# A fused pooling and state-space layer: the sample's scan factors computed at once for all heads, and three sums of squares as products of two parts

## The chip, the cores and the metric

The kernel runs on one core of a Trainium2 chip. The metric is the device time of one execution, in microseconds (us). The engines that matter are TensorE (PE: matmuls, with PEld for its weight loads), VectorE (DVE), ScalarE (ACT) and GpSimd (POOL). SyncE (SP), ACT and POOL also issue DMA transfers. Each engine takes its instructions in an order that is fixed when the kernel is built; where one depends on another engine or on a transfer, it waits for a semaphore.

## The reference, cut to what matters

One layer is computed for two requests that share the weights: a prompt of 256 tokens and a sample of 32 tokens that continues a running stream. All 288 tokens (NT) go through the projections side by side. The part that the change touches is the scan:

```python
xn   = rmsnorm(x, norm_mix_pre)
proj = xn @ w_in                      # u_pool | z | xBC | dt
xbc  = silu(causal_dwconv(xbc))       # -> xs (32 heads of 64), B, C (2 groups)
acum = cumsum(dt * A)                 # per head
lmat = exp(acum_t - acum_s), t >= s   # per head: the "factors"
y    = (lmat * (C B^T)) @ (dt * xs)   # within a request
y   += exp(acum) * (C @ h0)           # sample: state carried in
y    = (y + D * xs) * silu(z)
y    = y * rsqrt(mean(y * y) + eps) * norm_g        # per group of 16 heads
mix  = concat[pool, y] @ w_out
...                                   # then norm, ConvFFN, norm
```

Weights are float32. On the chip every weight tile and every left factor is split into a high part (`hi`, the float32 rounded to the matmul's fp32r type) and the rest (`lo`), and a product is three fp32r matmuls: hi·hi, hi·lo and lo·hi.

## The kernel before, in words

Activations lie with channels over the 128 partitions and the 288 tokens along the free axis. `project()` streams a weight matrix in groups of 256 columns; for each it takes four weight tiles of 128x1024 (`raw`, by DMA on SP), splits them (`whi` by ACT in L138, `wlo` by DVE in L139), and `mm3` issues 24 matmuls of 128x288 per tile (L145 to L147). The order of instructions on each engine is made by a scheduler when the kernel is built; `issue_after`, `high_priority` and `keep_in_program_order` bend it. PE runs matmuls of the projections nearly from end to end; the scan's work is fitted between them.

The scan works on groups of four heads, here called fours (q = 0 to 7). After certain projections (the tables `SCAN_IN` and `SCAN_OUT`, not changed) `scan(i)` does one or both of:

- `four_in(q)`: loads the four's running sums `gb`, its inputs `xw` and its state `h0t`, and forms `ce` and the factors `m`. `m` holds for each of the four heads 256 columns for the prompt's first half, 128 for its second, and 32 for the sample, 416 in all. Twelve Relus (L497: per head 128x256, 128x128 and 128x32), one Exp over 128x1664 (L500) and one product with `cbt` (L502, DVE) make it. `m`, `xw` and `ce` have two buffers each, so the third four's `m` takes the place of the first's.
- `four_out(q)`: sixteen matmuls (L524) in four rounds k: k = 0 and 1 read the prompt's part of `m`, k = 2 the sample's part, k = 3 the state's part (`ce` with `h0t`). They are kept in program order on PE. The first time it runs, two fours go out, q = 0 and q = 1.

`last_in[0]` is the latest DVE instruction that brought a projection's result out of PSUM. `gate_rstd` sums the squares over channels as one float32 matmul with a constant matrix `mean` (L533), twice in the scan; the same is done once more in the last stage (`psum_m`).

```python
four_out(q, ys[2 * n : 2 * n + 2], *got, after=None if n else ready[-1][1][-1])
```

This line of `scan` lets a four's matmuls start only after the product of the last prepared four (`got`, L502) in the order.

## Time and profile before

| What | Value |
|---|---|
| Time, median of 3 runs | 1232.44 us (1232.38 to 1233.84) |
| Profiled execution, its own time | 1231.95 us |
| Span of the profile (first to last instruction) | 1230.2 us |
| PE busy | 1223.2 us, 10037 matmuls |
| DVE busy | 888.5 us |
| ACT busy | 672.2 us |
| POOL busy | 277.8 us |
| First scan output on PE | from 130.12 us |

Times in the trace count from the span's start. A timeline row gives the start, the time taken, the engine, the line of the kernel, what is written from what, the shape and the count; in brackets stands how long the engine had been idle before and what released it. Matmuls overlap, so the distance between two starts is what one costs. A row with a count joins like instructions in sequence. A float32 matmul (not fp32r) appears as two records.

## The change

1. The sample's factors leave `m`, which shrinks from 4 x 416 to 4 x 384 columns (eight Relus in place of twelve, Exp and product over 1536 columns). They are computed once for all eight fours in a tile `ms` (128 x 8 x 32), with the 32 sample tokens of four heads over the 128 partitions: four DMAs on POOL, a subtraction on DVE, Relu and Exp on ACT, three products on DVE, and then four copies on ACT into blocks on the diagonal of a zeroed tile `msz` (32x256 each). Round k = 2 of `four_out` reads `msz` and a small tile `xw_s` of its own.
2. `four_in` is cut in two: the loads stay, the rest becomes `four_mul`. For q = 0 it is called one projection later, behind the third last weight split (`splits[-3]`).
3. The three sums of squares are two fp32r matmuls each, with a high part (a copy on ACT) and the rest (a subtraction on DVE), by `sum_parts`. The constant `mean_r` is a copy on ACT at the kernel's start.

The diff, cut to its core:

```diff
+    mean_r = const.tile([P, P], F32R, name="mean_r")
+    act.activation(mean_r, mean, AF.Copy)
+    def sum_parts(p_, src, pool_, name, last_=True):
+        a = [pool_.tile([P, NT], F32R, tag="sq", bufs=2, name=name) for _ in range(2)]
+        act.activation(a[0], src, AF.Copy)
+        dve.tensor_tensor(a[1], src, a[0].bitcast(F32), op=ALU.subtract)
+        return [(p_, mean_r, a[i], i == 0, last_ and i == 1) for i in range(2)]
...
+    for j in range(4):
+        pool.dma_start(
+            out=ms[NS * j : NS * (j + 1)],
+            in_=g_d.rearrange("(q j) c -> j q c", j=4)[j, :, 384:].unsqueeze(0).broadcast_to([NS, 8, NS]),
+        )
+    def sample_factors():
+        each = lambda t: t.unsqueeze(2).broadcast_to([P, 8, NS])
+        with tc.issue_after(last_in[0].ins):
+            dve.tensor_tensor(ms, each(tok_s[:, 0, :]), ms, op=ALU.subtract)
+            act.activation(ms, ms, AF.Relu)
+            act.activation(ms, ms, AF.Exp, scale=-1.0)
+            for gi in range(2):
+                q4 = slice(4 * gi, 4 * gi + 4)
+                dve.tensor_tensor(ms[:, q4], ms[:, q4], cbs[:, gi : gi + 1, :].broadcast_to([P, 4, NS]), op=ALU.mult)
+            dve.tensor_tensor(ms, ms, each(tok_s[:, 1, :]), op=ALU.mult)
+            for j in range(4):
+                r_ = slice(NS * j, NS * (j + 1))
+                act.activation(msz[r_, j], ms[r_], AF.Copy)
...
-        xw = mp.tile([P, 3, 2 * P], F32, tag="xw", bufs=2, name="xw")
-        sp.dma_start(out=xw[:, 0:2, :], in_=xs_d[:NP_, c].rearrange("(b p) c -> p b c", p=P))
-        sp.dma_start(out=xw[:, 2, :], in_=xs_d[NT - P :, c])
+        xw = mp.tile([P, 2, 2 * P], F32, tag="xw", bufs=2, name="xw")
+        sp.dma_start(out=xw, in_=xs_d[:NP_, c].rearrange("(b p) c -> p b c", p=P))
+        xw_s = mp.tile([P, 64], F32, tag="xw_s", bufs=2, name="xw_s")
+        sp.dma_start(out=xw_s, in_=xs_d[NP_:, c].rearrange("s (j c) -> j s c", j=4))
...
-                for b, (lo_, hi_) in enumerate(((0, 256), (256, 384), (384, MW))):
+                for b, (lo_, hi_) in enumerate(((0, 256), (256, CW))):
...
-                    ops.append((y[:, 256:], xw[:, 2, c], m[:, j, 384:], True, False))
+                    ops.append((y[:, 256:], xw_s, msz[:, j, q, :], True, False))
...
-        ins = pe.matmul(p_, mean, gsum[t], start=True, stop=True)
+        for o, w_, v_, go, end in sum_parts(p_, gsum[t], mp, "gsplit"):
+            ins = pe.matmul(o, w_, v_, start=go, stop=end)
...
+    def four_next(after):
+        q, tiles = loads.pop(0)
+        ready.append((q, four_mul(q, *tiles, after)))
     def scan(i):
+        if loads:
+            four_next((*splits[-3], last_in[0]))
         if i in SCAN_OUT:
...
         if i in SCAN_IN:
-            ready.append((q, four_in(q)))
+            loads.append((q, four_in(q)))
+            if i > 5:
+                four_next((last_in[0],))
+        if i == 6:
+            sample_factors()
```

How the order of instructions changes is shown at three places around the first scan output. In these rows `m`, `xw`, `ce`, `h0t` and `py` are the factors, inputs, state factors, states and results of a four, and `[waits X]` names the engines or transfers whose semaphore an instruction waits for. The line numbers are those of each kernel's own source.

On ACT, before, these rows start with the first Relu of q = 2, whose `m` takes the buffer of q = 0:

```order
L497 ACTIVATE m<-gb,tok 128x256 [waits PE_49]
L497 ACTIVATE m<-gb,tok 128x128
L497 ACTIVATE m<-gb,tok 128x32
L497 ACTIVATE m<-gb,tok 128x256
L497 ACTIVATE m<-gb,tok 128x128
L497 ACTIVATE m<-gb,tok 128x32
L487 ACTIVATE ce<-gb 128x128 [waits PE_49]
```

On ACT, now, from the same Relu on:

```order
L558 ACTIVATE m<-gb,tok 128x256 [waits PE_49]
L558 ACTIVATE m<-gb,tok 128x128
L558 ACTIVATE m<-gb,tok 128x256
L558 ACTIVATE m<-gb,tok 128x128
L558 ACTIVATE m<-gb,tok 128x256
L558 ACTIVATE m<-gb,tok 128x128
L558 ACTIVATE m<-gb,tok 128x256
L558 ACTIVATE m<-gb,tok 128x128
L561 ACTIVATE m<-m 128x1536 [waits Activation_49]
L520 ACTIVATE msz<-ms 32x256 [waits DVE_49]
L520 ACTIVATE msz<-ms 32x256 x3
L548 ACTIVATE ce<-gb 128x128 [waits PE_49]
```

The four copies into `msz` stand behind all eight Relus and the Exp of q = 2, and the first of these Relus waits for PE.

On PE, before, the first four's output, between two projections:

```order
L524 MATMUL py<-m,xw 64x256 [waits DMAHW0_49]
L524 MATMUL py<-m,xw 64x256 x3
L524 MATMUL py<-m,xw 64x128 x4
L524 MATMUL py<-m,xw 64x32 [waits DMAHW1_49]
L524 MATMUL py<-m,xw 64x32 x3
L524 MATMUL py<-ce,h0t 64x32 [waits DMAHW7_49]
L524 MATMUL py<-ce,h0t 64x32 x3
```

On PE, now:

```order
L585 MATMUL py<-m,xw 64x256 [waits DMAHW0_49]
L585 MATMUL py<-m,xw 64x256 x3
L585 MATMUL py<-m,xw 64x128 x4
L585 MATMUL py<-msz,xw_s 64x32 [waits DMAHW1_49,Activation_49,Pool_49]
L585 MATMUL py<-msz,xw_s 64x32 [waits Activation_49] x3
L585 MATMUL py<-ce,h0t 64x32 [waits DMAHW7_49]
L585 MATMUL py<-ce,h0t 64x32 x3
```

The eight matmuls of k = 0 and 1 stand where they stood; the four of k = 2 now each wait for a copy on ACT.

On DVE, before, ahead of the first scan output, from a result brought out of PSUM (`ebuf`) to the split of a weight (`wlo`):

```order
L360 TENSOR_TENSOR ebuf_674<-acc,rstd 128x256 [waits PE_49]
L361 TENSOR_TENSOR ebuf_674<-acc,rstd 128x32
L490 TENSOR_TENSOR ce<-ce,bc 128x128
L493 TENSOR_TENSOR xw<-xw,tok 128x768 [waits DMAHW7_49,DMAHW0_49]
L502 TENSOR_TENSOR m<-m,cbt 128x1664 [waits DMAHW3_49]
L139 TENSOR_TENSOR wlo<-raw,whi 128x1024 [waits Activation_49]
```

On DVE, now, between the same two:

```order
L372 TENSOR_TENSOR ebuf_676<-acc,rstd 128x256 [waits PE_49]
L373 TENSOR_TENSOR ebuf_676<-acc,rstd 128x32
L551 TENSOR_TENSOR ce<-ce,bc 128x128
L554 TENSOR_TENSOR xw<-xw,tok 128x512 [waits DMAHW0_49]
L563 TENSOR_TENSOR m<-m,cbt 128x1536
L551 TENSOR_TENSOR ce<-ce,bc 128x128
L554 TENSOR_TENSOR xw<-xw,tok 128x512 [waits DMAHW7_49]
L563 TENSOR_TENSOR m<-m,cbt 128x1536 [waits DMAHW3_49]
L511 TENSOR_TENSOR ms<-tok_s,ms 128x256 [waits DMASW2_49,DMASW3_49,DMASW1_49,DMASW0_49]
L140 TENSOR_TENSOR wlo<-raw,whi 128x1024 [waits Activation_49]
```

The products of q = 0 moved down to those of q = 1, and with the subtraction for `ms` stand ahead of this `wlo`.

## What the change was predicted to do

> **What bounds the kernel now.** I read the page's busy shares, clock row and chain first, then the waits of PE, then the timelines of PE, ACT and DVE around the places that the change touches. The page:

> ```profile
> span 1230.2 us, 25184 instructions
> PE 1223.2 (99%) x10037; PEld 1212.8 (99%) x10037; DVE 888.5 (72%) x1488; ACT 672.2 (55%) x1013; POOL 277.8 (23%) x428
> PEclk9999999999999999999999999999999999999999
> PE 91%; DVE 3%; ACT 3%; issue 1%; DMA 1%; ACTq 0%; DVEq 0%
> ```

> The waits of PE (what waits, for whom, us in total, times, longest):

> ```profile
> PE idle L261 <- PEq L1316: 0.8, 1, 0.8
> PE psum_f L1223 <- DVE ar L1198: 0.5, 1, 0.5
> PE acc L147 <- DVE wlo L139: 0.4, 1, 0.4
> PE acc L292 <- DVE xs L290: 0.4, 1, 0.4
> PE acc L147 <- DVE wlo L302: 0.4, 1, 0.4
> PE y_ps L1256 <- DVE ar L1250: 0.3, 1, 0.3
> ```

> PE is the bound from end to end: 99% busy, 91% of the chain, the clock full in every slice, and only 2.8 us of waiting in the whole span. So work taken from DVE and ACT is worth nothing by itself; what counts is PE's own matmuls, and whether PE gets a new wait. At 99% any new wait of PE lengthens the span by its full length.

> **Part 1, the sample's factors: the first scan output.** On PE nothing is saved: a 64x32 product stays a 64x32 product, with `msz` for the end of `m`. But round k = 2 now waits for four copies on ACT, and the order of ACT puts these behind eight Relus and the Exp of q = 2. The first of these Relus writes into the buffer of q = 0's `m`, so it waits for PE's last k = 1 matmul of q = 0, the one right ahead of k = 2. So PE must stand still while ACT does all that. Before, the Relus waited in the same way, but nothing that PE needed then was behind them. When PE gets there, from its timeline (weight matmuls, then the first four):

> ```profile
> 127.33 0.29 PE L147 MATMUL acc<-xn,wlo 128*128 128x288 f32 x1
> ...
> 129.90 0.29 PE L147 MATMUL acc<-xn,wlo 128*128 128x288 f32 x1
> 130.12 1.73 PE L524 MATMUL py<-m,xw 128*64 128x256 f32 x24
> 131.67 0.41 PE L524 MATMUL py<-ce,h0t 128*64 128x32 f32 x8
> 131.90 0.63 PE L524 MATMUL py<-m,xw 128*64 128x256 f32 x4
> ```

> From 127.33 to 129.90 there are 21 steps, so 0.1224 us a step. Each float32 product is two records: x24 are the twelve products of k = 0 to 2, x8 the four of k = 3. The latter take 131.90 - 131.67 = 0.23 us; the four of k = 2 have the same size, so k = 2 begins at 131.44 and its last product at 131.61. The last k = 1 product, issued just before 131.44, is done some 0.2 us later, at about 131.64 (estimate from the records' length). What ACT's pieces take, by ACT's timeline:

> ```profile
> 4.66 0.72 ACT L301 ACTIVATE whi<-raw 128x256 fp32r<-128x256 f32 x2 [0.41 <-DMA raw<-in_w_first]
> 7.03 1.03 ACT L301 ACTIVATE whi<-raw 128x256 fp32r<-128x256 f32 x3 [1.20 <-DMA raw<-in_w_first]
> 110.02 1.57 ACT L500 ACTIVATE m<-m 128x1664 f32<-128x1664 f32 x1
> 111.51 0.39 ACT L497 ACTIVATE m<-gb,tok 128x128 f32<-128x128 f32 x1
> ...
> 112.47 0.31 ACT L497 ACTIVATE m<-gb,tok 128x32 f32<-128x32 f32 x1
> 112.68 1.04 ACT L138 ACTIVATE whi<-raw 128x1024 fp32r<-128x1024 f32 x1
> ...
> 132.27 1.90 ACT L497 ACTIVATE m<-gb,tok 128x256 f32<-128x256 f32 x6
> 134.08 0.29 ACT L487 ACTIVATE ce<-gb 128x128 f32<-128x128 f32 x1
> ```

> - Eight Relus: six (two heads of 256, 128, 32) go from 132.27 to 134.08, 0.905 a head. The 32-wide one is 112.68 - 112.47 = 0.21, so a head now costs 0.695, and four 2.78.
> - Exp: 111.51 - 110.02 = 1.49 for 1664 columns, 1.38 for 1536.
> - Four copies of 32x256: no row has this form. The nearest is a 128x256 copy, 0.41 alone and 0.31 for each further one (1.03 - 0.72): 1.34. From below, each at the 0.21 of the 32-column Relu: 0.84.

> The last copy ends at 131.64 + 2.78 + 1.38 + 1.34 = 137.14, and its product, which had started at 131.61, is **5.53 us** late. From below 5.0 (cheap copies). From above 6.2: ACT may reach the first Relu no earlier than in the row at 132.27, 0.63 after 131.64. What DVE and ACT do in that time (splits of the next weights) finishes early and is no loss.

> **The products moved on DVE.** q = 0's products now stand with q = 1's in front of one `wlo`. DVE's rows before:

> ```profile
> 122.62 0.28 DVE L490 TENSOR_TENSOR ce<-ce,bc 128x128 f32<-128x128 f32 x1
> ...
> 123.69 1.88 DVE L502 TENSOR_TENSOR m<-m,cbt 128x1664 f32<-128x1664 f32 x1
> 125.49 1.22 DVE L139 TENSOR_TENSOR wlo<-raw,whi 128x1024 fp32r<-128x1024 f32 x1
> ```

> `ce` and `xw` took 1.07 and `m` 1.80; with 512 and 1536 columns that is 0.2 + 0.6 + 1.67 = 2.47 for a four, so twice 2.47 and 0.33 for the subtraction of `ms` (128x256) make 5.27 against 2.87: this `wlo` ends 2.40 later than 126.71, if DVE starts at the same time. PE first reads it at 127.33, two matmuls later in the new order, 127.57: slack 0.86, so a wait of 1.5 us at worst. But DVE no longer does q = 0's 2.87 us earlier on and so reaches this place earlier, unless it waits there for PE's result: 0 at best. I take 0.2, near the lower end, since the time is given back to the same queue. Two later places (near 160 and 179) have the same shape with one four: 0 to 0.7 together, by the half of this wait; I take 0.1. Sum +0.3.

> **Other steps of part 1 with one answer.** The four loads of `ms` stand on POOL's queue ahead of writes of `xs_d`, and the loads of `xw_s` on SP's among the weights'; both are needed only at about 126 and 131, more than 10 us later, so 0. The copies of `tok_s`, `b_s4`, `dec_s` and `tri_s`, the memset and the Relu and Exp of `ms` lie on ACT and POOL (55% and 23% busy) ahead of 126; 0, and if the Relu of `ms`, which waits for DVE, holds a split behind it, it is inside the 1.5 above. Later fours have shorter products on DVE and ACT.

> **Part 2, the sums of squares.** One of them on PE, with the weight matmuls behind it:

> ```profile
> 212.50 0.65 PE L533 MATMUL psum_g<-gsum,mean 128*128 128x288 f32 x2
> ...
> 213.10 0.29 PE L146 MATMUL acc<-xn,whi 128*128 128x288 f32 x1
> 213.23 0.29 PE L145 MATMUL acc<-xn,whi 128*128 128x288 f32 x1
> 213.92 0.39 PE L147 MATMUL acc<-xn,wlo 128*128 128x288 f32 x1 [0.41 <-DVE wlo L139]
> 214.15 0.29 PE L145 MATMUL acc<-xn,whi 128*128 128x288 f32 x1
> ```

> From 212.50 to 213.10 lie the sum and one weight matmul, 0.60; two fp32r products and that one are three steps, 0.367. So 0.235 less each, **-0.71** for three; 0 if PE must wait for the split instead.

> **Waits that may go.** The rows above show one: 213.23 to 214.15 is 0.92 for two steps of 0.245, 0.67 waited for `wlo`. The other:

> ```profile
> 151.88 0.29 PE L146 MATMUL acc<-xn,whi 128*128 128x288 f32 x1
> 152.26 0.39 PE L147 MATMUL acc<-xn,wlo 128*128 128x288 f32 x1
> 152.48 0.29 PE L145 MATMUL acc<-xn,whi 128*128 128x288 f32 x1
> ```

> 0.60 for two steps, so 0.36. Both are waits for a `wlo` close behind a product of 1664 columns, which is now shorter and, behind a standstill, has time in hand: **-1.03** together if both go, 0 if neither. More than 0.71 + 1.03 = 1.74 can't be gained, since the other waits are not touched.

> **Part 3, the start.** ACT now loads its table and copies `mean_r` between its two loads of `x`:

> ```profile
> 1.25 0.45 ACTq L256 DMA_DIRECT2D xT<-in_x  x1
> 1.74 1.28 ACT L257 ACT_TABLE_LOAD   x1 [1.74 <-PEq L1316]
> xT<-in_x ACTq DMA_DIRECT2D x1, 144.0 KB, 3.5
> ```

> The second load is issued some 1.5 us later (1.28 for the table and 0.2 for the copy) and lands at about 6.3 instead of 1.25 + 3.5 = 4.8. PE's next weights land only at 7.03 (ACT's row above), so 0; 0.5 at most, if `x`'s second part is wanted first.

> **Sum.** 5.53 + 0.3 - 0.71 - 1.03 = +4.1 against the profiled execution of 1231.95 us (its span and 1.75 around it): 1236.0. This execution is 0.49 below the median of the runs, 1232.44, so by the median 1236.5, +0.33%. This case's own range: from 5.0 + 0 - 1.74 = +3.3 (1235.7) to 6.2 + 0.8 - 1.4 = +5.6 (1238.0).

> **Rivals.**

> *The stall costs twice: PE runs at half speed after it.* PE's first matmuls show such a state:

> ```profile
> 0.85 2.90 PE L261 MATMUL idle<-const-float32-1.0 128*128 128x128 f32 x12 [0.85 <-PEq L1316]
> ...
> 5.74 0.50 PE L145 MATMUL acc<-xn,whi 128*128 128x288 f32 x1
> L292 PE MATMUL acc<-xs,raw 128*128 128x288 f32 x4 | 2.0, 644 | 0.4 <-DVE xs L290 0.4
> L533 PE MATMUL psum_g<-gsum,mean 128*128 128x288 f32 x4 | 1.3, 406 | 0.0
> ```

> A float32 record of 128x288 takes 644 ns at the start and 406 in the sums; the fp32r matmul at 5.74 still takes 0.50, later ones 0.29. So PE begins slow, from 0.85 to about 5.7 with 0.4 of waiting, some 4.4 us, while the page's clock digit says full speed there. If a standstill of 5.5 us brings that back, 4.4 us at half rate cost 2.2: 1238.7 (1237.8 to 1239.7). Against it: the trace has no later standstill over 0.5 us, so it can't show one. [...]

> *A wait on DVE ahead of the scan.* If DVE gets to q = 0's products no earlier than before, the full 1.5 us at 127.57 come on top, with the stall unchanged (its start moves with PE): 1236.5 + 1.3 = 1237.8. For it: DVE waits there for PE's result (`ebuf`). Against it: 2.87 us of its earlier work are gone.

> *Not slower: no long standstill.* If the order's wait is met early, because the Relu that waits is satisfied before PE reaches k = 1 (q = 2's `m` in a buffer of its own), the copies end before 131.44 and only the gains are left: 1232.44 - 1.74 + 0.3 = 1231.0, within 0.2%. It decides as soon as the standstill is under 2.46 + 1.44 = 3.9 us, since 2.46 us are 0.2%, about what runs of this kernel can tell from no change. Against it: the order shows the slot wait before and now, and in the row at 132.27 the Relus did begin only after k = 1.

> **How the numbers follow.** Stall with full speed 0.45; with half speed 0.31; DVE's wait on top 0.12; no long standstill, or one cut under 3.9, 0.12. The first gives the time, 1236.5. The range goes from 1234.6, where the last case's upper part ends, to 1239.3, in the half-speed case's upper part; some 0.10 are left out below, 0.06 above. Slower by over 0.2% (above 1234.90) are the first three, 0.86 with a little lost to low ends, given to the last: slower 0.85, same 0.12, faster (below 1229.98) 0.03.

> **What would show it.** In the changed trace: PE idle about 5 us at 131.6, ahead of `py<-msz,xw_s`, released by ACT L520; eight Relus, an Exp and four copies without a gap on ACT between; matmul steps of 0.122 right behind it (0.24 if the half-speed case holds, for some 4 us); no wait for `wlo` near 152 and 213; three sums without float32 records. Wrong I am if copies into `msz` lie before 131, or if PE's waits stay below 4 us in total.

## The result, and the profile after

| | before | changed |
|---|---|---|
| Median | 1232.41 us (1230.74 to 1233.84, 4 runs) | 1238.64 us (1238.0 to 1240.47, 4 runs) |
| Profiled execution, its span | 1231.95, 1230.2 us | 1238.0, 1236.3 us |

The ratio is 1.0059, 95% interval 1.0046 to 1.0071: slower by 0.59%. The forecast was +0.33%, 1236.5 us, with a range up to 1239.3; the median lies near the range's upper end, and the ratio times 1232.44 (1239.7) just above it. The direction and the place were right; the size was too small.

The page of the changed kernel:

```profile
span 1236.3 us, 25196 instructions
PE 1224.2 (99%) x10037; PEld 1214.4 (98%) x10037; DVE 887.5 (72%) x1494; ACT 670.8 (54%) x1000; POOL 287.2 (23%) x436
PEclk9999899999999999999999999999999999999999
PE 93%; DVE 2%; DMA 2%; ACT 1%; issue 1%; SPq 0%; ACTq 0%; DVEq 0%
```

One slice in 40 has a digit 8 in the clock row, the fifth, from 124 to 155 us: the first scan output lies there. Two waits of PE in the changed kernel that the kernel before does not have (the second lies at 127.6):

```profile
PE py L585 <- issue: 4.8, 1, 4.8
PE acc L149 <- DVE wlo L140: 0.9, 1, 0.9
```

PE's timeline at both places (the last row is the first matmul of the next projection, at 133.77 before):

```profile
127.57 0.39 PE L149 MATMUL acc<-xn,wlo 128*128 128x288 f32 x1 [0.92 <-DVE wlo L140]
...
130.22 1.52 PE L585 MATMUL py<-m,xw 128*64 128x256 f32 x16
136.58 1.58 PE L585 MATMUL py<-msz,xw_s 128*64 128x32 f32 x7 [4.84 <-issue]
...
137.97 0.29 PE L585 MATMUL py<-msz,xw_s 128*64 128x32 f32 x1
...
141.52 0.39 PE L147 MATMUL acc<-xn,whi 128*128 128x288 f32 x1
```

ACT's timeline shows what PE waited for, row by row as the prediction had listed it. The first `msz` product follows the first copy (136.08), and the last one (137.97) the fourth, which ends at 137.79:

```profile
131.79 2.87 ACT L558 ACTIVATE m<-gb,tok 128x256 f32<-128x256 f32 x8 [0.53 <-PE py L585]
134.69 1.48 ACT L561 ACTIVATE m<-m 128x1536 f32<-128x1536 f32 x1
136.08 1.71 ACT L520 ACTIVATE msz<-ms 32x256 f32<-32x256 f32 x4
```

And the granted clock, in four stretches (PE busy, PEld, DVE, ACT, POOL, then the clock, share of DMA, GB/s):

```profile
130.62:134.03 3.41, 1.12 (x16) 0.66 (x12) 3.41 (x10) 2.88 (x8) 2.25 (x4) 1.00 0.96 312
134.04:137.45 3.41, 0.85 (x5) 0.61 (x5) 3.41 (x8) 3.31 (x7) 3.41 (x6) 0.50 1.02 299
137.45:140.86 3.41, 3.40 (x27) 3.26 (x29) 3.41 (x6) 1.53 (x4) 2.75 (x4) 0.50 0.84 319
140.86:144.00 3.14, 3.14 (x41) 3.10 (x38) 2.78 (x10) 2.81 (x8) 1.25 (x3) 1.00 1.01 364
```

The clock fell to 0.50 at 134.04, 2.3 us after PE's last k = 1 product, while PE stood still, and came back at 140.86, two stretches of 3.41 us later. Between, the rest of the scan ran at half speed, but for its last 0.7 us.

Where the 6.0 us between the two profiled executions went, by the starts of like matmuls in the two timelines (for the sums of squares three shifts of 0.22 to 0.25; the start by the weight matmul at 28.8 us before, 27.7 now):

| Place | Forecast | Measured |
|---|---|---|
| Start of the kernel | 0 | -1.09 |
| Wait for `wlo` at 127.6 | +0.2 | +1.19 |
| Standstill at the first scan output | +5.53 | +6.2 |
| Half speed behind it | 0 (rival: 2.2) | +1.4 |
| Two later places | +0.1 | 0 |
| Waits near 152 and 213 | -1.03 | -1.03 |
| Three sums | -0.71 | -0.69 |
| Sum | +4.1 | +6.0 |

The scan took 133.77 - 130.12 = 3.65 us before and 141.52 - 130.22 = 11.30 now. From the last `msz` product (137.97) to the end are 3.55 us, where before 2.13 lay: 1.4 for the half speed; the other 6.2 are the standstill up to that product.

## The experiments

Each ran beside the kernel before on the same chip. Ratios are to that kernel, with 95% intervals; 0.1% is 1.2 us.

**e1: the sample's factors earlier.**

```diff
-        with tc.issue_after(last_in[0].ins):
+        with tc.high_priority():
             dve.tensor_tensor(ms, each(tok_s[:, 0, :]), ms, op=ALU.subtract)
...
-        if i == 6:
+        if i == 5:
             sample_factors()
```

> The changed kernel with sample_factors called one projection earlier, with high priority and without its gate, so that the four copies into msz stand on ACT ahead of the Relus of q = 2; all else as changed. Theory (the standstill at the first scan output comes from the copies' place in the order, and the slow matmuls behind it from the standstill): both go, 7.65 us less, about 1231 us, with the wait of 1.2 us for wlo at 127.6 still there. Rival (PE waits there for something else that the change brought, the small transfer of xw_s or the zeroing of msz): the standstill stays and the time stays near 1238.6. Rival (the products with msz or the smaller m are slow in themselves): no standstill, but the first scan output still takes well over 3.65 us, and the time is near 1232.5.

Measured: 1231.23 us against 1231.09, ratio 1.000 (0.9991 to 1.0009). The standstill is gone, and the scan has its old length. PE's timeline of e1:

```profile
128.64 0.39 PE L149 MATMUL acc<-xn,wlo 128*128 128x288 f32 x1 [1.46 <-DVE wlo L140]
...
131.28 1.52 PE L585 MATMUL py<-m,xw 128*64 128x256 f32 x16
132.64 0.38 PE L585 MATMUL py<-msz,xw_s 128*64 128x32 f32 x8
```

The first `msz` product starts 1.36 us after the scan begins, at a granted clock of 1.00 (from 129 to 134 us); `xw_s`, the zeroed blocks and the small products cost nothing, so both rivals fall. The wait for `wlo` stayed, 1.46 us, and it eats what the rest of the change gains. This edit moves both the copies on ACT and the products on `ms` on DVE; e7 separates them.

**e7: only the copies ahead of the Relus.** The edit moves the Relus of q = 2 behind the copies and leaves DVE's order up to the last product on `ms` as it was.

```diff
+    blocks = []
...
-                act.activation(msz[r_, j], ms[r_], AF.Copy)
+                blocks.append(act.activation(msz[r_, j], ms[r_], AF.Copy))
...
-                four_next((last_in[0],))
+                four_next((last_in[0], *blocks[-1:]))
```

> The changed kernel with one edit: the four_mul calls after sample_factors are issued behind the last copy into msz, so that on ACT the four copies stand ahead of q = 2's Relus. On DVE the last product on ms stays where it was, behind two weight splits, two results from PSUM and two convolution steps; in the changed kernel's trace it ended at 135.0. Theory of the prediction (the standstill comes from the Relus and the Exp in front of the copies): it goes, and the time falls by 7 us or more, to 1231. Second theory, from the changed kernel's trace (the last product on ms on DVE ends at 135.0 and would by itself hold PE): the first msz product starts at about 135.2, PE stands still for 3.4 us in place of 4.8, the clock still falls to half, and the time is 1.4 us less than the changed kernel's, plus what the later Exp of q = 2 costs at the second scan output.

Measured: 1239.25 us against 1230.99, ratio 1.0071 (1.0057 to 1.0085): no faster than the changed kernel. The rows of e7's timelines, of DVE, ACT and PE in order of time:

```profile
134.83 0.41 DVE L519 TENSOR_TENSOR ms<-ms,tok_s 128x256 f32<-128x256 f32 x1
...
135.28 1.73 ACT L522 ACTIVATE msz<-ms 32x256 f32<-32x256 f32 x4 [3.78 <-DVE ms L519]
...
135.79 1.58 PE L587 MATMUL py<-msz,xw_s 128*64 128x32 f32 x7 [3.82 <-issue]
...
137.18 0.29 PE L587 MATMUL py<-msz,xw_s 128*64 128x32 f32 x1
...
141.25 0.61 PE L147 MATMUL acc<-xn,whi 128*128 128x288 f32 x1
```

With the Relus out of the way, ACT itself waits 3.78 us for DVE's last product on `ms`, PE stands still for 3.82 in place of 4.84, and the clock falls as before (0.50 from 135.54 to 142.30). So the prediction's cause was real but not alone: a second one, nearly as long, stood behind it on DVE. The shorter standstill should still have gained 1.0 us (the second theory said 1.4), and the trace shows where that went. From the last `msz` product (137.18) to the next projection (141.25) are 4.07 us, with 2.13 before and 3.55 in the changed kernel, and the first matmuls of the projection are slow too: 2.4 us of half speed in place of 1.4, since the stretch of slow clock is as long as before (6.8 us) but more of the work lies in it. Near 163 and 182 PE loses another 0.5 against the other profiles. Moving the DVE product alone was not tried; by the order, the copies would still stand behind the Relus and the Exp. In the changed kernel's trace that product lies at 134.59, ahead of the copies at 136.08:

```profile
134.59 0.41 DVE L517 TENSOR_TENSOR ms<-ms,tok_s 128x256 f32<-128x256 f32 x1
```

**e2 and e2s: PE kept busy in the standstill.** Idle float32 products (64x256 of constants, into a PSUM tile not yet in use) are put between k = 1 and k = 2 of q = 0: 26 in e2, 12 in e2s.

```diff
...
+        if q == 0:
+            ops[8:8] = [(spare, mean[:, 0:64], bc[2][:, 0:NP_], True, True)] * 26
         for y, w_, v_, go, end in ops:
...
```

> The changed kernel with 26 idle float32 products (64x256, into a PSUM tile that is not yet in use) on PE between rounds k = 1 and k = 2 of the first four, so that PE works through the standstill; nothing else is moved around it. Theory (the matmuls behind the standstill are slow because PE stood still): 26 x 0.22 = 5.7 us of the 6.3 are filled, the copies come as before, and the rest of the scan runs at full speed: 1.4 us less, about 1237.2. Rival (they are slow for their own reasons, or from what ACT and DVE do at that time): still 3.5 us from the last msz product to the next projection, and 1238.6.

Measured: 1244.85 us, ratio 1.0113 (1.0099 to 1.0127). The expectation missed by its own sizing: 0.22 us is one of the two records of a product, so 26 products took 11.2 us and made PE late themselves. But the stretch behind them, from 142.50 to 145.00, ran at a clock of 1.00.

> The changed kernel with 12 idle products instead of the 26 of e2, which turned out to take 0.43 us each: 5.2 us, so PE still stands for 1.1 us ahead of the first msz product. Theory (the clock falls to half because PE stands still for over 2 us): the clock stays at full speed through the scan, 1.4 us less than the changed kernel run beside it. Rival (the slow clock does not depend on it): the same time as the changed kernel.

Measured: 1238.45 us, ratio 1.0061 (1.0047 to 1.0076); the changed kernel beside it (e6) 1239.25, 1.0062. The times don't tell them apart. The traces do: in e2s PE worked through the standstill, and the clock stayed at 1.00:

```profile
131.50:136.50 5.00, 5.00 (x33) 3.32 (x29) 5.00 (x12) 4.44 (x10) 4.28 (x8) 1.00 0.95 330
136.50:140.50 4.00, 3.73 (x52) 3.12 (x50) 4.00 (x7) 2.29 (x7) 3.83 (x4) 1.00 0.83 272
```

Between the last matmul ahead of the scan and the first behind it, e2s lost 6.2 us against before, e6 7.9 and the first profile 7.65: 1.4 to 1.7 us are the half speed, and the idle products take it away. e2s lost 1.0 of that again near 378 us, where PE waited 0.82 for a `wlo` behind a product that waits for a transfer; such waits stand in some profiles and not in others (below).

**e6: the changed kernel again.**

> The changed kernel once more, on the same chip as these. Expected: 6 to 7.5 us over the kernel before; the standstill at 131.7 again 4.8 us long, and the clock at half speed from 1.7 to 5 us after its beginning on, until a window of about 3.4 us in which PE works again has passed. What the first matmul of the projections starts at (5.28 before, 5.88 and 6.02 in other runs) tells how much of the earlier profile's gain at the start is chance.

Measured: 1239.25 us against 1231.75, ratio 1.0062 (1.005 to 1.0074): 7.5 us more, the upper end of what was expected. The clock fell 2.8 us after PE's last k = 1 product (132.16), where it was 2.3 in the first profile and 3.5 in e7; the 1.7 to 5 us were the author's estimate. The same picture, in e6's PE timeline:

```profile
137.00 1.58 PE L585 MATMUL py<-msz,xw_s 128*64 128x32 f32 x7 [4.84 <-issue]
```

And in its clock, by stretches that begin and end where the clock changed, at 134.97 and 141.80:

```profile
131.56:134.97 3.41, 0.60 (x10) 0.36 (x6) 3.41 (x9) 2.88 (x9) 2.77 (x5) 1.00 0.98 329
134.97:138.38 3.41, 1.35 (x8) 0.98 (x10) 3.41 (x8) 3.14 (x6) 3.41 (x5) 0.50 0.81 230
138.39:141.80 3.41, 3.41 (x34) 3.41 (x36) 3.41 (x7) 1.22 (x4) 2.24 (x4) 0.50 1.01 344
```

**e3: the first run at once.** Part 2 of the change undone.

```diff
-            if i > 5:
+            if i > 4:
                 four_next((last_in[0],))
```

> The changed kernel with one part undone: four_mul of q = 0 is called at once, as before, and not behind the weights' splits. In its order the products of q = 0 stand two splits earlier on DVE, and the copies into msz stand ahead of q = 2's Relus on ACT, though still behind the last product on ms, which waits behind two splits on DVE. Theory: the wait for wlo at 127.6 goes (1.2 us), and the standstill shrinks to what the last product on ms is late, 0.5 to 3 us, too short to slow the clock: 1231 to 1233. Rival (the wait at 127.6 comes from the subtraction for ms, or from ACT, not from the products of q = 0): the wait stays at about 1 us.

Measured: 1233.18 us against 1231.09, ratio 1.0014 (1.0005 to 1.0022). The wait at 127.6 is gone, the granted clock over the span is 0.999 (0.997 in the changed kernel), and the scan is 1.6 us longer than before, inside the expected 0.5 to 3; the time is 0.2 above the expected 1231 to 1233. That up to 3 us would be too short to slow the clock was the author's estimate and is not shown: e2's wait of 2.02 us, below, had the clock at 0.50 behind it. The expected gain of 1.2 turned into a new wait one projection earlier, in e3's PE timeline:

```profile
115.12 0.39 PE L149 MATMUL acc<-xn,wlo 128*128 128x288 f32 x1 [1.32 <-DVE wlo L140]
```

DVE's product of q = 0 stands there ahead of this `wlo`; in the kernel before it stood behind it. So holding the first run back moved a wait of this size from 113 to 127.6; it didn't remove it.

**e5: early factors and the first run at once** (e1 and e3 together).

> The changed kernel with both: the sample's factors one projection earlier with high priority, and four_mul of q = 0 at once. Theory: standstill, slow clock and the wait at 127.6 all go: 1238.6 - 7.65 - 1.2 = 1229.8, about 2.6 under the kernel before, of which 0.7 are the sums and 1.0 the waits near 152 and 213. Rival (those two waits went only because the standstill gave DVE time): they come back, 1230.8. Rival (the early factors put a new wait on DVE or ACT one projection earlier): a wait for wlo before 127, 1231 to 1232.

Measured: 1231.04 us against 1231.09, ratio 1.000 (0.9991 to 1.0008). No standstill, but PE waits 0.50 for a `whi` and 1.33 for the `wlo` near 113, as the second rival had it. The wait for `wlo` is in e3 too, without the early factors, so only the one for `whi` can be theirs.

**t3: the first run behind one split, without the other gate.** e1's edit, and:

```diff
-            four_next((*splits[-3], last_in[0]))
+            four_next(splits[-3])
```

> The changed kernel with the sample's factors one projection earlier, as in e1, and the products of q = 0 held back only behind the third last weight split, without last_in[0], which had put them behind the result of the next projection. On DVE they then stand behind the wlo that was late at 112.9 in e3 and e5, and not in front of the one that is late at 127.6 in the changed kernel and e1. Theory (each of those waits of 1.2 to 1.5 us is a four's products in front of one wlo): no wait for wlo over 0.5 us, and what is left of the change are the sums (0.7) and the waits near 152 and 213 (1.0): 1.7 us less than before, ratio 0.9986. Rival (DVE and ACT are so full between 100 and 130 us that the work only moves to another split): one wait of 1 us or more at another place, ratio 1.000.

Measured: 1229.85 us against 1231.75, ratio 0.9984 (0.9976 to 0.9993), faster than the kernel before and as expected. PE's waits in t3 hold no `wlo`:

```profile
PE idle L273 <- PEq L1389: 0.8, 1, 0.8
PE acc L304 <- DVE xs L302: 0.6, 1, 0.6
PE psum_f L1296 <- DVE ar L1271: 0.5, 1, 0.5
PE y_ps L1329 <- DVE ar L1323: 0.3, 1, 0.3
```

On DVE the product of q = 0 now lies between two splits of which neither is urgent, and only one four stands ahead of the split that PE wanted at 127.6:

```profile
108.66 1.23 DVE L140 TENSOR_TENSOR wlo<-raw,whi 128x1024 fp32r<-128x1024 f32 x1 [0.18 <-ACT whi L139]
110.32 1.76 DVE L563 TENSOR_TENSOR m<-m,cbt 128x1536 f32<-128x1536 f32 x1 [0.44 <-ACT m L561]
...
122.27 1.75 DVE L563 TENSOR_TENSOR m<-m,cbt 128x1536 f32<-128x1536 f32 x1
123.94 1.22 DVE L140 TENSOR_TENSOR wlo<-raw,whi 128x1024 fp32r<-128x1024 f32 x1
```

**e4: the sums alone**, in the kernel before.

> The kernel before with the three sums of squares changed alone (mean_r, sum_parts and the three places). Expected: each sum takes 0.37 us with the weight matmul behind it and not 0.60, so 0.7 us less than before, ratio 0.9994; the waits for wlo at 152 and 213 stay, since DVE's products keep their 1664 columns. Rival (the split into two parts makes PE wait at the first of them): about 0, with a wait at psum_g.

Measured: 1231.91 us against 1231.75, ratio 1.000 (0.9992 to 1.0009); 0.7 us is less than this can tell. In the trace the sum takes two steps with no wait ahead of it, and a wait of another kind stands at 378 us:

```profile
212.37 0.43 PE L544 MATMUL psum_g<-gsplit,mean_r 128*128 128x288 f32 x2
...
378.43 0.39 PE L147 MATMUL acc<-mixp,wlo 128*128 128x288 f32 x1 [1.01 <-DVE wlo L139]
```

The shifts against before are about -0.22 at each of the three sums, as forecast. But also -0.28 near 152 and -0.68 near 213: those waits shrank here too, though DVE's products kept their 1664 columns. Ahead of the one near 213, ACT had reached the Exp of that four at 207.88 in place of 209.23, in another order around the sum. So these waits shrink without the shorter products; why they do is not shown.

## Why the prediction was right or wrong

**Right: the bound, the place and the chain.** PE stood still at the first scan output, its products released one by one by the four copies, and the rows on ACT were those of the sum: Relus from 131.79 (131.64 forecast), Exp from 134.69 to 136.08 (1.39, forecast 1.38). Against the forecast of 137.14 the last copy ended at 137.79: the Relus took 2.90 for 2.78, and the copies 1.71 for 1.34. **Mis-sized: the copies.** A 32x256 copy takes 0.41 with 0.43 from start to start, where the nearest row, 128x256 copies, gave 0.31; fewer partitions were not cheaper. With the Relus and the hand-over to PE the standstill was 6.2 for 5.53, so this term was 0.7 short.

**Incomplete: what the copies waited for.** The step that puts the copies "behind eight Relus and the Exp of q = 2" took ACT's queue as the only cause. e7 showed that DVE's last product on `ms`, behind other work until 135.0, would have held PE for 3.8 us by itself. It changes no term of the sum, but the remedy that the prediction's own rival named, a buffer for q = 2's `m`, would by e7 leave PE standing for these 3.8 us (it was not tried).

**Wrong: "Stall with full speed", the largest miss.** This is the step that failed: the sum puts the clock behind the standstill at nothing, with chances of 0.45 for full speed and 0.31 for half, on the ground that the trace before has no standstill over 0.5 us to show a fall. Half speed came in both profiles of the changed kernel and cost 1.4 and 1.7 us, under the 2.2 that the rival gave. e2s shows that the standstill is the cause: with PE kept busy through it, the clock stays at 1.00. In the stretch of 3.41 us ahead of the fall PE had worked 1.12 us in the changed kernel, 0.60 in e6 and nothing in e7. The bounds of this rival, 1237.8 to 1239.7, are narrower than the first case's (1235.7 to 1238.0) moved up by 2.2, and the prediction gives no reason for it.

**Wrong: the wait on DVE, 0.2.** It took the low end of 0 to 1.5, on the ground that DVE no longer had q = 0's 2.87 us earlier on. DVE did come earlier, but only by 1.6 us (the result `ebuf` at 120.59 in place of 122.19), and 1.09 of these are the earlier start of this execution, so against PE it gained 0.5. Most of the freed time went into waits for ACT (2.11 us in the rows of the kernel before, 3.91 in those of the changed one, which follow):

```profile
109.76 1.23 DVE L139 TENSOR_TENSOR wlo<-raw,whi 128x1024 fp32r<-128x1024 f32 x1 [1.46 <-ACT whi L138]
...
111.63 1.89 DVE L502 TENSOR_TENSOR m<-m,cbt 128x1664 f32<-128x1664 f32 x1 [0.65 <-ACT m L500]
```

```profile
108.54 1.23 DVE L140 TENSOR_TENSOR wlo<-raw,whi 128x1024 fp32r<-128x1024 f32 x1 [2.40 <-ACT whi L139]
...
111.83 1.23 DVE L140 TENSOR_TENSOR wlo<-raw,whi 128x1024 fp32r<-128x1024 f32 x1 [0.80 <-ACT whi L139]
...
114.15 1.23 DVE L140 TENSOR_TENSOR wlo<-raw,whi 128x1024 fp32r<-128x1024 f32 x1 [0.71 <-ACT whi L139]
```

From there to the late `wlo` DVE works without a gap. This place cost 1.0 to 1.7 us in the six profiles that have this order (1.19 in the first, 1.7 in e1). The rival that priced it had it as an alternative to the half speed; both came at once, and none of the cases held their sum.

**Right in size by luck: the waits near 152 and 213.** -1.03 was measured, but e4 has nearly the same (-0.96) with long products, so the reason given is not needed. **Right: the sums**, -0.69 for -0.71. **Not foreseen: the start.** It was 1.09 us earlier in the first profile, and by the same matmul 0.50 earlier in e6, but 0.77 and 0.15 later in e3 and e4, whose first instructions are like the changed kernel's. PE's first weight matmuls show why, first of the changed kernel and then of e3:

```profile
5.28 0.39 PE L147 MATMUL acc<-xn,whi 128*128 128x288 f32 x1
5.51 0.29 PE L148 MATMUL acc<-xn,whi 128*128 128x288 f32 x1
```

```profile
6.02 0.85 PE L147 MATMUL acc<-xn,whi 128*128 128x288 f32 x1
6.67 0.45 PE L148 MATMUL acc<-xn,whi 128*128 128x288 f32 x1
6.91 0.45 PE L147 MATMUL acc<-xn,whi 128*128 128x288 f32 x1
```

In e3 PE is still at half speed at 6.91 (0.45 a matmul, 0.24 from start to start), in the changed kernel no longer at 5.51 (0.29 and 0.12). The trace's record of the granted clock begins, at 1.00, at 9.09 in e3, and for the same changed kernel at 4.33 in the first profile and at 5.27 in e6: it differs between executions, and the gain at the start is luck, no effect of the change. It hid a third of the miss: the copies, the half speed and the wait on DVE came to 3.1 us more than forecast, the early start took 1.1 off, and 2.0 are left. The table of ACT and its second load of `x` cost nothing that can be seen.

## What to carry to other kernels

When the order puts something that PE needs behind an instruction that waits for PE, price the standstill by the rows behind that instruction, and then look for the next producer up the chain: removing one of two causes in series gains at most the difference, and in e7 not even that. Half speed behind a standstill has to be reckoned with: behind those of 4.84 us (the changed kernel, e6) and 3.82 (e7) the clock stood at 0.50 for two stretches of 3.41 us, behind e2's wait of 2.02 for one, and in the stretch with e1's wait of 1.46 and the next it was 1.00. How much work falls into the slow stretches decides the price (1.4 to 2.4 us here). Work that must stand ahead of a weight's split is best placed by the slack of that split: the same 2.5 us of products cost 1.0 to 1.7 us at one place of this kernel, 1.6 at another (e3) and nothing at a third (t3), and there the whole change became a small gain.

## What was not expected of the hardware

The clock fell after a stretch in which PE had worked a third of the time (1.12 of 3.41 us in the changed kernel, to 134.03). It also fell once without a long standstill: in e2, near 390 us, PE waited 2.02 us for a `wlo`, and the next stretch ran at half speed:

```profile
387.94:391.35 3.41, 1.39 (x11) 1.18 (x11) 3.41 (x3) 1.06 (x1) 0.00 (x0) 1.00 0.01 5
391.35:394.76 3.41, 3.41 (x16) 3.41 (x15) 2.42 (x3) 0.00 (x0) 0.00 (x0) 0.50 0.69 209
```

There PE had been busy for 1.39 of 3.41 us. In e1 the stretch with the wait of 1.46 us, 3.41 us long and in step with that execution's changes of the clock, left it at 1.00 (in the changed kernel's first profile the changes, at 4.33, 134.04, 140.86 and 1236.54, lie 38, 2 and 321 times 3.413 us apart):

```profile
126.09:129.50 3.41, 1.95 (x16) 1.73 (x16) 3.41 (x7) 1.39 (x2) 2.92 (x1) 1.00 0.00 0
```

The last matmuls of t3 come closer. PE works 1.49 us of the first of these stretches, and the clock is still at 1.00 through the next, which is wholly idle; it falls only behind that one, at 1229.37:

```profile
1222.54:1225.95 3.41, 1.49 (x6) 0.99 (x6) 1.60 (x3) 1.15 (x3) 0.00 (x0) 1.00 0.83 308
1225.96:1229.36 3.40, 0.00 (x0) 0.00 (x0) 0.00 (x0) 0.00 (x0) 0.00 (x0) 1.00 0.22 84
```
